# A hybrid decoder step on one core: the prompt's compressed branch beside the compression, in a buffer that later holds half of u

## The chip, the cores and the metric

One core of a Trainium2 chip runs the kernel. The metric is the device time of one execution in microseconds; the kernel before takes 1119.47 us (median of 3 runs, 1118.45 to 1124.41).

## What is computed

The kernel is one inference step of a one-layer hybrid decoder for T = 320 tokens in float32: a prompt of 256 and 8 samples of 8 tokens with caches. Shortened, the reference is:

```python
q, kv, ag, z, xbc, dt, mg = split(rmsnorm(x) @ w_in)         # 1024 -> 6 kinds of columns
A = NSA(q, kv, ag)      # three branches per head, each its own softmax, summed with sigmoid gates
#   o_c: 15 compressed blocks of 32 tokens (a small MLP over the raw keys and values: "compression")
#   o_s: selected 64-token blocks       o_w: a sliding window of 512
M = Mamba2(z, xbc, dt)  # causal conv of width 4, chunked SSD scan, gated norm
h = x + (sigmoid(ga) * (A @ Wa) + sigmoid(gm) * (M @ Wm)) @ w_out
y = h + HierMoE(rmsnorm(h))   # 4 groups of 8 experts: best group, then the best 2 experts in it
```

For the prompt, o_c is softmax(q KC + bias) VC over the compressed keys KC, one softmax row for each token, each of 16 heads; the bias carries ALiBi and the mask.

## The kernel before, in words

Tokens lie on the free axis (320 columns) wherever a projection is computed: a 256-column block of w_in comes in as `w`, ACT and DVE split it into a high and a low part (`whl`, `split`, L342 and L343), and PE multiplies by `xh` and `xl` in three products of 128x128 by 128x320 per 128 rows (`mm`, 24 for a tile of 128 output columns). These projections are the filler of the whole first half: the generator `st_fill` yields 16 conv tiles (`post_xbc`), 8 z tiles (`post_z`), then merge gates and the two output branches. A function `_drive(main, fill, rate)` runs main generators and the filler on a virtual clock (each `yield` is a cost in ns; the filler's are multiplied by a rate), which sets the order in which the program is written; the scheduler of the tile framework then fixes each engine's order. Nothing is reordered at run time: an engine whose next instruction waits holds all that stands behind it.

The stages, with their places in the trace: k, v, q projections (0 to about 92 us); `st_cmp`, the compression of eight samples and the prompt (to about 225); `st_prompt`, the prompt's attention (to about 310); `st_att`, the samples' attention (to about 421); `st_ssd` (to about 562); output projection and router; `ph_moe` from about 645 on, whose weights come over the SP queue through a ring of buffers.

- The head of `st_prompt` is the compressed branch: 16 products of q with `KC` into a PSUM tile (`at`), bias added on DVE (L944), row maximum (L945, L946), subtract (L947), multiply by the slopes (L951), Exp on ACT (L952), sum (L953), reciprocal (L776, L777), gates (L956), scaling (L959), 8 transposes on PE and two copies (L965) into `PcT`. All of it works in `Pc`, one of three buffers of the tag `PP`.
- The main loop of `st_prompt` has 16 turns (head pair r, query tile qt): `probs` multiplies q2 and K2 (`at<-K,q`, in high and low parts), adds the mask with a row maximum on DVE (`ttr`, L782; L994 scales the maxima) and takes four Exps on ACT (L998); `norm` scales (DVE, and POOL at L1008); `out` transposes `PP`, copies, and multiplies by the values (`pv`) together with `PcT`.
- `ph_b_setup` makes K2 (ACT L646, DVE L648) just before; `q2_parts` makes the two parts of q2 (ACT L655, POOL L656).
- `st_ssd` begins by transposing `u`, the conv's x half, which the filler wrote to memory (`ud`) and `ph_c_setup` loads back on ACT's DMA queue (L1153).
- `st_att` begins with DMAs on the SP queue: a constant row `cB` (L790), `P` (L794), then the windows (`wraw`, L799).
- `back` in the MoE transposes the one-hot rows `oh` of an expert and, with three products with N = 3 in float32 each, fetches the expert's coefficients `cr`; six small copies put them in place.

Of the kernel before, what the change touches and what calls it, by code (L numbers as in the profile page):

```python
# [9 lines left out]
F32 = mybir.dt.float32  # L10
# [22 lines left out]
T = 320  # L33
# [132 lines left out]
class _Body:  # L166
# [288 lines left out]
    def ph_a(s):  # L455
# [174 lines left out]
    def ph_b_setup(s):  # L630
# [39 lines left out]
    def st_cmp(s):  # L670
# [14 lines left out]
        for pr in range(4):  # L685
            n = 256 if pr else 292
            for kv in range(2):
# [54 lines left out]
                if pr == 0:  # L742
# [59 lines left out]
    def st_att(s):  # L802
# [4 lines left out]
        def one(b):  # L807
# [65 lines left out]
            def ptb(srcs):  # L873
# [3 lines left out]
                t = s.tl(P_, [128, 4, 128], F32, "PT", bufs=8)  # L877
# [20 lines left out]
            tn = s.tl(P_, [128, 4, 128], F32, "PT", bufs=8)  # L898
# [29 lines left out]
    def st_prompt(s):  # L928
# [3 lines left out]

        Pc = s.Pc
        Pv = Pc.rearrange("p (a n) -> p a n", n=32)
        stt = s.tl(P_, [128, 3, 32], F32, "cst")
        KC = s.KC.rearrange("p g n -> p (g n)")
        for qt in range(2):
            p = s.ps("at", [128, 512])
            if qt == 1:
                s.q2_parts(0, 2)  # L940
            for r in range(8):
                n = 96 if r < 7 else 64
                s.mm(p[:, r * 64:r * 64 + n], s.qT[:, r, qt * 128:(qt + 1) * 128], KC[:, 0:n], True, True)
            nc.vector.tensor_tensor(Pc[:, qt * 512:(qt + 1) * 512], p, Pc[:, qt * 512:(qt + 1) * 512], op=OP.add)  # L944
        nc.vector.tensor_reduce(stt[:, 0], Pv, axis=AX.X, op=OP.max)  # L945
        nc.vector.tensor_scalar(stt[:, 0], stt[:, 0], -1e20, None, op0=OP.max)  # L946
        nc.vector.tensor_tensor(Pv, Pv, stt[:, 0, :, None].to_broadcast([128, 32, 32]), op=OP.subtract)  # L947
        psl = s.ca("psl")
        for qt in range(2):
            v = Pv[:, qt * 16:(qt + 1) * 16]  # L950
            nc.vector.tensor_tensor(v, v, psl[:, :, None].to_broadcast([128, 16, 32]), op=OP.mult)  # L951
        nc.scalar.activation(Pc, Pc, AF.Exp)  # L952
        nc.vector.tensor_reduce(stt[:, 1], Pv, axis=AX.X, op=OP.add)  # L953
        s.recip_gate(None, stt[:, 1], None)
        for qt in range(2):
            nc.vector.tensor_tensor(stt[:, 2, qt * 16:(qt + 1) * 16].rearrange("p (r g) -> p r g", g=2),  # L956
                                    stt[:, 1, qt * 16:(qt + 1) * 16].rearrange("p (r g) -> p r g", g=2),
                                    gp[:, qt, :, :, 0].rearrange("p g r -> p r g"), op=OP.mult)
        nc.vector.tensor_tensor(Pv, Pv, stt[:, 2, :, None].to_broadcast([128, 32, 32]), op=OP.mult)  # L959
        PcT = s.tl(P_, [128, 8, 128], F32, "PcT")  # L960
        for hh in range(2):
            p = s.ps("tp", [128, 4, 128])
            for u in range(4):
                s.tr(p[:, u], Pc[:, (hh * 4 + u) * 128:(hh * 4 + u + 1) * 128])
            nc.scalar.copy(PcT[:, hh * 4:hh * 4 + 4], p)  # L965
        yield 4500
        sl = _slopes()
        nsl = s.ca("nsl")
        def probs(r, qt):
# [89 lines left out]
    def st_fill(s):  # L1059
# [27 lines left out]
        def late():  # L1087

            n = 344
            if pend:  # L1090
# [17 lines left out]
                if f % 4 == 3:  # L1108
                    q = f // 4
                    pt = s.ps("tp", [32, 4, 128])  # L1110
                    for k in range(4):
                        s.tr(pt[:27, k], ctail[:, q * 4 + k])
                    cv = s.tl(P, [27, 512], F32, "cv")
                    nc.scalar.copy(cv, pt[:27].rearrange("p a b -> p (a b)"))
                    nc.sync.dma_start(s.O["conv_prompt"][:, q * 512:(q + 1) * 512], cv[0:3])
                    nc.sync.dma_start(s.O["conv_sample"].rearrange("b w c -> (b w) c")[:, q * 512:(q + 1) * 512], cv[3:27])

        def post_z(m):
            def post(p):
# [5 lines left out]
                nc.sync.dma_start(s.zd[m // 2][m % 2], z)  # L1125
                if m == 7:
# [18 lines left out]

# [951 lines left out]
```

## Time and profile before

| | before |
|---|---|
| time, median of 3 runs | 1119.47 us |
| the profiled execution: its own time, its span | 1119.53 us, 1117.8 us |
| PE busy | 1057.1 us (95%) |
| DVE busy, ACT busy | 618.2 us (55%), 409.6 us (37%) |
| moved by DMA | 298.01 MB, 267 GB/s on average |

Busy time is the time in which an engine has an instruction running; "idle before, releaser" is the time that it stood still ahead of an instruction, with what ended that. PEclk is the granted clock of TensorE as a share of its full 2.4 GHz; a window at 0.50 ran at the lower level, 1.2 GHz, throughout. Outside the span lie 1.7 us of the execution.

### The profile page before, as it was taken

The numbers are of one execution on the slowest core, as the hardware profiler recorded it, in microseconds if no ns is written. First come the engines' busy times: TensorE is split into PE (matmuls) and PEld (weight loads), VectorE is DVE, ScalarE is ACT, GpSimd is POOL, SyncE is SP. The second block draws the span as 40 slices with busy tenths as digits, with TensorE's granted clock in tenths as the row PEclk, the third lists the DMA queues.
The fourth block names the chain that finished last, engine by engine and source line by source line (L and its number), as shares of the span: only waits on it lengthen the run. The fifth ranks groups of instructions, "written<-read, shape, count | busy, mean of one in ns | idle before, by whom it ended". The sixth has DMA issues, their size and how long they took to land.

```text
span 1117.8 us, 18377 instructions
## 1 busy us (share of the span) xinstructions
PE 1057.1 (95%) x6743; PEld 728.9 (65%) x6743; DVE 618.2 (55%) x1686; ACT 409.6 (37%) x959; POOL 85.0 (8%) x115
## 2 busy tenths in 40 slices
PE   6998999969999998999999989999999999999997
PEld 6898899957776787777899944354444444435333
DVE  4467777788867774578876532333434333333324
ACT  4446565677745452545545511110101010101101
POOL 3102000042200001024100000000000000000000
PEclk8999999989999998999999999999999999999999
DMA  7844555511266656584579969999999999999995
GB/s 213 229 139 141 164 153 155 149 56 55 87 181 204 196 153 191 155 229 91 138 267 342 375 211 411 413 414 413 411 412 414 413 414 413 412 412 414 413 413 197
DMA packets 141742, 298.01 MB, mean 267 GB/s; under 512 B 14918, under 2 KB 93222, under 8 KB 133970
## 3 DMA queue, kind: packets, MB, share of 16 engines
q1 hardware_dynamic: 135146, 283.34, 70.7%
q0 software_dynamic: 2688, 7.91, 2.3%
q10 hardware_dynamic: 3816, 5.56, 1.6%
q8 instruction: 55, 0.90, 0.3%
q14 instruction: 37, 0.30, 0.1%
HBM read 279.63 MB, written 15.29 MB: 264 GB/s over the span
## 4 chain that ended last, share of the span: by engine, by line


## 5 line engine op out<-in xcount | busy, mean ns | idle before, releaser
L215 PE MATMUL mm<-xh,whl 128*128 128x320 f32 (+1 forms) x1008 | 248.8, 326 | 7.6 <-ACT whl L342 4.4
L215 PEld LDWEIGHTS mm<-xh,whl 128*128 128x128 f32 (+1 forms) x1008 | 173.5, 191 | 21.1 <-issue 7.9
L215 PE MATMUL mm<-wr,xeT 128*64 128x512 f32 x752 | 171.8, 595 | 4.8 <-DMA wr<-in_w_exp_up 3.0
L215 PE MATMUL mm<-xl,whl 128*128 128x320 f32 (+1 forms) x504 | 162.9, 323 | 0.0
L215 PEld LDWEIGHTS mm<-wr,xeT 128*64 128x64 f32 x752 | 53.5, 137 | 109.8 <-issue 103.6
L215 PE MATMUL po<-wr,ehT 128*64 128x512 f32 (+1 forms) x448 | 118.5, 580 | 4.2 <-DMA wr<-in_w_exp_down 4.2
L343 DVE TENSOR_TENSOR whl<-w,whl 128x1024 fp32r<-128x1024 f32 (+1 forms) x79 | 96.0, 1217 | 23.7 <-ACT whl L342 22.5
L1805 DVE SCALAR_TENSOR_TENSOR eth<-eth,mm 128x256 f32<-128x256 f32 x31 | 13.1, 421 | 170.6 <-ACT eth L1804 170.6
L342 ACT ACTIVATE whl<-w 128x1024 fp32r<-128x1024 f32 (+1 forms) x79 | 83.1, 1055 | 45.8 <-PE mm L215 38.5
L215 PEld LDWEIGHTS mm<-xl,whl 128*128 128x128 f32 (+1 forms) x504 | 96.3, 191 | 3.3 <-issue 1.6
L1804 ACT ACTIVATE eth<-mm,cb 128x256 f32<-128x256 f32 x31 | 14.7, 475 | 201.0 <-PE mm L215 201.0
L215 PEld LDWEIGHTS po<-wr,ehT 128*64 128x64 f32 x448 | 37.3, 137 | 72.3 <-issue 60.3
L1858 DVE TENSOR_TENSOR ht<-sc,ht 128x512 f32<-128x512 f32 (+3 forms) x99 | 61.7, 665 | 38.7 <-PE sc L215 38.2
L215 PE MATMUL mm<-ah,whl 128*128 128x320 f32 x256 | 63.9, 322 | 0.0
L346 DVE SCALAR_TENSOR_TENSOR olo<-po,cb,ohi 128x512 fp32r<-128x512 f32 (+1 forms) x33 | 24.2, 734 | 49.7 <-ACT ohi L345 49.7
L1780 ACT ACTIVATE ohT<-tp 128x320 fp32r<-128x320 f32 x16 | 7.0, 437 | 106.1 <-PE sc L215 98.3
L215 PEld LDWEIGHTS mm<-ah,whl 128*128 128x128 f32 x256 | 43.9, 188 | 2.0 <-issue 0.7
L215 PE MATMUL tp<-oh,hh 128*128 128x256 f32 x192 | 42.2, 292 | 0.0
L215 PE MATMUL sc<-ohi,ohT 128*128 128x512 f32 (+3 forms) x99 | 41.5, 421 | 0.2
L345 ACT ACTIVATE ohi<-po,cb 128x512 fp32r<-128x512 f32 (+1 forms) x33 | 22.2, 674 | 53.1 <-PE po L215 53.1
L215 PE MATMUL mm<-al,whl 128*128 128x320 f32 x128 | 39.6, 309 | 0.0
L215 PEld LDWEIGHTS tp<-oh,hh 128*128 128x128 f32 x192 | 32.9, 188 | 9.0 <-issue 8.1
(491 smaller groups left out, 1895.0 us busy)
## 6 DMA issues: line engine op xcount, KB each, us to landing
wr<-in_w_exp_down SPq DMA_DIRECT2D x50, 1024.0 KB
wr<-in_w_exp_gate SPq DMA_DIRECT2D x98, 512.0 KB
wr<-in_w_exp_up SPq DMA_DIRECT2D x98, 512.0 KB
w<-in_w_in SPq DMA_DIRECT2D x23, 1024.0 KB
raw<-in_cache_kv SPq DMA_DIRECT2D x112, 128.0 KB
w<-in_w_exp_down SPq DMA_DIRECT2D x10, 1024.0 KB
whl<-in_w_exp_gate SPq DMA_DIRECT2D x20, 512.0 KB
whl<-in_w_exp_up SPq DMA_DIRECT2D x20, 512.0 KB
```

The costliest lines, as they stand in the source:

```text
L215: return s.nc.tensor.matmul(out, lhsT, rhs, start=start, stop=stop, skip_group_check=True)
L342: s.last_split = [nc.scalar.activation(hi, src, AF.Copy), nc.vector.tensor_tensor(lo, src, hi.bitcast(F32), op=OP.subtract)]
L343: nc.vector.tensor_tensor(lo, src, hi.bitcast(F32), op=OP.subtract)]
L345: nc.scalar.activation(hi, src, AF.Copy, scale=scale)
L346: nc.vector.scalar_tensor_tensor(lo, src, scale, hi.bitcast(F32), op0=OP.mult, op1=OP.subtract)
L1780: nc.scalar.activation(t, p[:, 0:T], AF.Copy)
L1804: nc.scalar.activation(hv, g, AF.Tanh, scale=hrs)
L1805: nc.vector.scalar_tensor_tensor(hv, hv, 1.0, g, op0=OP.add, op1=OP.mult)
L1858: nc.vector.tensor_tensor(y, ps[:m], y, op=OP.add)
```

## The change

It moves the compressed branch of the prompt out of `st_prompt` into a generator of its own, `st_pc`, which runs beside `st_cmp`; puts `Pc`, `PcT` and the small `cst` into one tile `ux` of pool pU, which is later allocated again for `u`, loaded by `load_x` on the SP queue; makes parts 2 to 7 of q2 later, each pair behind an Exp; saves SBUF at five places to make room; and in `back` takes `cr` in two fp32r parts. Cut to its core ("..." is what is left out; the body of `st_pc` between the products and the transposes is the removed code, word for word but for the tile and a `yield` after each step or two):

```diff
 def post_q(r):
-    t = s.tl(s.pst, [128, T], F32, "qt", bufs=2)
+    t = s.tl(s.pst, [128, T], F32, "kvx", bufs=2)
...
-    si.append(s.tl(s.pst, [24, 1024], F32, "si", bufs=2))
+    si.append(s.tl(s.pst, [128, 1024], F32, "xscr", bufs=3)[:24])
...
+    def ph_pc_setup(s):
+        t = s.tl(s.pU, [128, 8 * T], F32, "ux")
+        s.Pc = t[:, 0:1024]
+        s.PcT = t[:, 1024:2048].rearrange("p (a b) -> p a b", b=128)
+        s.cst = t[:, 2048:2144].rearrange("p (a b) -> p a b", b=32)
...
+        nc.sync.dma_start(s.Pc, s.I["cB"][:, o:o + n])
+    def st_pc(s):
+        yield lambda: "kc" in s.flags
...
+        for qt in range(2):
+            p = s.ps("tp", [128, 512])
+            for r in range(8):
+                n = 96 if r < 7 else 64
+                s.mm(p[:, r * 64:r * 64 + n], s.qT[:, r, qt * 128:(qt + 1) * 128], KC[:, 0:n], True, True)
+            nc.vector.tensor_tensor(Pc[:, qt * 512:(qt + 1) * 512], p, Pc[:, qt * 512:(qt + 1) * 512], op=OP.add)
+            yield 3000
...
+        for hh in range(2):
+            p = s.ps("tp", [128, 4, 128])
+            for u in range(4):
+                s.tr(p[:, u], Pc[:, (hh * 4 + u) * 128:(hh * 4 + u + 1) * 128])
+            nc.scalar.copy(s.PcT[:, hh * 4:hh * 4 + 4], p)
+            yield 3000
-    def q2_parts(s, a, b):
+    def q2_parts(s, a, b, after=None):
...
+            with s.tc.issue_after(after.ins) if after is not None else nullcontext():
+                s.nc.scalar.activation(hi, q, AF.Copy)
...
-        t = s.tl(s.pB, [128, 292], F32, "gt", bufs=2)[:, :n]
+        t = s.tl(s.pB, [128, 292], F32, "gt")[:, :n]
...
-                t = s.tl(P_, [128, 4, 128], F32, "PT", bufs=8)
+                t = s.tl(P_, [128, 4, 128], F32, "PT", bufs=6)
...
     def st_prompt(s):
-        Pc = s.Pc
...
+        PcT = s.PcT
+        s.q2_parts(0, 2)
...
         for r in range(8):
             for qt in range(2):
+                cur = probs(r, qt)
                 if r % 2 == 0 and qt == 1 and r < 6:
-                    s.q2_parts(r + 2, r + 4)
-                cur = probs(r, qt)
+                    s.q2_parts(r + 2, r + 4, s.last_exp)
...
-                if f % 4 == 3:
+                if f % 2:
...
-                    cv = s.tl(P, [27, 512], F32, "cv")
+                    cv = s.tl(P, [27, 256], F32, "cv")
...
         def post_z(m):
...
+                if "prompt" in s.flags:
+                    s.load_x()
...
+    def load_x(s):
+        if not hasattr(s, "u"):
+            s.u = s.tl(s.pU, [128, 8 * T], F32, "ux").rearrange("p (f t) -> p f t", t=T)
+            for k in range(2):
+                s.nc.sync.dma_start(s.u[:, 4 * k:4 * k + 4], s.ud[k].rearrange("f p t -> p f t"))
     def ph_c_setup(s):
+        s.load_x()
...
-        for k in range(2):
-            nc.scalar.dma_start(s.u[:, 4 * k:4 * k + 4], s.ud[k].rearrange("f p t -> p f t"))
...
+        s.crs = s.tl(P, [128, 3, 16, 2, 3], F32R, "crs")
+        s.split(s.crs[:, :, :, 0], s.crs[:, :, :, 1], s.cr)
...
-                mm(p[:, 384:387], o[i], s.cr[:, i, e // 2], i == 0, i == 2)
+                mm(p[:, 384:390], o[i], s.crs[:, i, e // 2].rearrange("p a b -> p (a b)"), i == 0, i == 2)
...
-                nc.vector.tensor_copy(cb[u, 0:1], p[u, 384 + a:385 + a])
+                nc.vector.tensor_reduce(cb[u, 0:1], p[u, 384 + a:390:3], axis=AX.X, op=OP.add)
...
-    _drive([s.st_cmp()], [fill], RATES[0])
+    s.ph_pc_setup()
+    _drive([s.st_cmp(), s.st_pc()], [fill], RATES[0])
...
     _drive([s.st_prompt()], [fill], RATES[3])
+    s.flags.add("prompt")
```

How the orders of the engines change, at three places. The names are those of the tiles; numbers behind them tell copies of a tile apart.

**PE where the prompt's attention begins.** Before, the first transposes of `PP` are those of the compressed branch (two rows of four), behind the products of three turns:

```order
L215 MATMUL at_2527<-K_317_2339,q_316_2338 128x512 x2
L215 MATMUL at_2608<-K_317_2339,q_316_2338 128x256 x4
L215 MATMUL at_2657<-K_317_2339,q_316_2338 128x512 x2
L215 MATMUL mm_4017<-xh_119,whl_3763 128x320 x2
L215 MATMUL mm_4017<-xl_120,whl_3763 128x320
L215 MATMUL mm_4017<-xh_119,whl_3763 128x320
L227 MATMUL tp_2389<-cA_109,PP_2336 128x128 x4
L227 MATMUL tp_2395<-cA_109,PP_2336 128x128 x4
L227 MATMUL tp_2446<-cA_109,ctail_1097 27x128 x4
```

In the change:

```order
L215 MATMUL mm_3741<-xh_119,whl_3621 128x320
L215 MATMUL at_2408<-K_323_2390,q_322_2389 128x256 x2
L215 MATMUL at_2476<-K_323_2390,q_322_2389 128x512 x2
L215 MATMUL at_2408<-K_323_2390,q_322_2389 128x256 x2
L215 MATMUL mm_3987<-xh_119,whl_3738 128x320
L215 MATMUL mm_3987<-xl_120,whl_3738 128x320
L215 MATMUL at_2479<-K_323_2390,q_322_2389 128x512 x2
L215 MATMUL at_2519<-K_323_2390,q_322_2389 128x256 x4
L215 MATMUL at_2615<-K_323_2390,q_322_2389 128x512 x2
L215 MATMUL at_2618<-K_323_2390,q_322_2389 128x512 x2
L215 MATMUL mm_3987<-xh_119,whl_3738 128x320 x2
L227 MATMUL tp_2501<-cA_109,PP_2406 128x128 x4
```

The products with `KC` and the eight transposes of the branch are gone from here (they now stand between the `hh` products of the compression), and the first transposes are those of the main loop's first turn, `PP_2406`. Ahead of the first `at<-K,q` stand 44 products of the filler since the last transposes of the compression.

**DVE in the compression, change.** The operations of the branch (on `ux`) stand between the conv's (`cvt`, `ut`) and the gelu's (`gt`, `gx`) of the compression:

```order
L671 TENSOR_TENSOR ux_984<-tp_1475,ux_984 128x512
L1114 SCALAR_TENSOR_TENSOR ut_2609<-raw_2607,cvt_2451 128x256
L673 TENSOR_REDUCE ux_984<-ux_984 128x32
L1115 SCALAR_TENSOR_TENSOR ut_2609<-raw_2607,cvt_2451 128x64
L674 TENSOR_SCALAR ux_984<-ux_984 128x32
L1090 MEMSET raw_2680 128x3
L676 TENSOR_TENSOR ux_984<-ux_984 128x1024
L714 SCALAR_TENSOR_TENSOR gt_1560<-gt_1560,gx_1558 128x256
L681 TENSOR_TENSOR ux_984<-ux_984,cA_11_110 128x512
L716 SCALAR_TENSOR_TENSOR gx_1558<-gt_1560,gx_1558 128x256
L681 TENSOR_TENSOR ux_984<-ux_984,cA_11_110 128x512
```

What was one block at the head of `st_prompt` is now spread over the second half of the compression, one step ahead of or behind each step of the other streams.

**ACT in the tail of st_ssd.** Before, one Tanh table serves the gates `gm`, and the table for Ln and Exp is loaded once behind them:

```order
L1477 ACTIVATE gm_5306<-mm_6384 128x320
L1350 ACTIVATE k_1002_6416<-at_6410 64x4x64
L1393 ACT_TABLE_LOAD
L1398 ACTIVATE ysq_6280<-ysq_6297 128x320
L1350 ACTIVATE k_1005_6437<-at_6431 128x512
L342 ACTIVATE whl_6457<-w_6299 128x1024
L342 ACTIVATE whl_6521<-w_6378 128x1024
```

In the change a third gate stands behind that load, and the tables are changed again from there on:

```order
L1503 ACTIVATE gm_5298<-mm_6370 128x320
L342 ACTIVATE whl_6399<-w_6335 128x1024
L1376 ACTIVATE k_1008_6434<-at_6428 64x4x64
L1419 ACT_TABLE_LOAD
L1376 ACTIVATE k_1011_6455<-at_6449 128x512
L1503 ACT_TABLE_LOAD
L1503 ACTIVATE gm_5298<-mm_6402 128x320
```

In the whole program the change has 18 rows of ACT_TABLE_LOAD where there were 11; the 7 new ones all stand from this place to the end of `st_ssd`. On the SP queue the first half of `u` now stands directly ahead of `cB`, `P` and the windows, and it writes the tile that the last `pv` of `st_prompt` reads.

## Rows read from the trace of the kernel before

**Rows 1.** Windows, head of st_prompt: length, busy PE PEld DVE ACT POOL, PEclk, DMA.
```profile
230.00:255.00 25.00, 13.67 (x70) 11.15 (x70) 23.14 (x53) 16.31 (x39) 14.48 (x10) 0.73 0.15 48
245.00:250.00 5.00, 2.05 (x6) 1.35 (x6) 5.00 (x21) 3.59 (x17) 0.41 (x1) 0.50 0.00 0
250.00:255.00 5.00, 4.18 (x19) 3.64 (x20) 5.00 (x13) 1.44 (x4) 2.17 (x2) 0.53 0.67 207
```
**Rows 2.** Waits of PE, 200 to 260 us: total, times, longest.
```profile
PE at L215 <- DVE pmx L782: 5.9, 2, 4.2
```
**Rows 3.** Timeline of PE there: start, us, instruction, [idle before].
```profile
225.29 0.46 PE L215 MATMUL mm<-xh,whl 128*128 128x320 f32 x2
226.61 0.46 PE L215 MATMUL mm<-xh,whl 128*128 128x320 f32 x2
227.05 3.68 PE L215 MATMUL at<-KC,qT 128*128 128x96 f32 x32
252.25 1.94 PE L227 MATMUL tp<-cA,PP 128*128 128x128 f32 x8 [0.21 <-DVE PP L959]
```
**Rows 4.** Timeline of ACT there.
```profile
224.68 1.28 ACT L440 ACT_TABLE_LOAD   x1
225.97 0.69 ACT L440 ACTIVATE cr<-tp,small 128x512 f32<-128x512 f32 x1
228.89 2.56 ACT L646 ACTIVATE K<-kvT 64x512 fp32r<-64x512 f32 x4
231.48 5.22 ACT L655 ACTIVATE q<-qT 64x512 fp32r<-64x512 f32 x8
244.72 0.40 ACT L998 ACTIVATE PP<-PP,pmx 128x128 f32<-128x128 f32 x1
```
**Rows 5.** Timeline of POOL there.
```profile
232.25 12.42 POOL L656 TENSOR_TENSOR q<-qT,q 64x512 fp32r<-64x512 f32 x8 [28.90 <-ACT q L655]
```
**Rows 6.** Timeline of DVE there.
```profile
229.78 2.78 DVE L648 TENSOR_TENSOR K<-kvT,K 64x512 fp32r<-64x512 f32 x4
232.59 1.29 DVE L944 TENSOR_TENSOR PP<-at,PP 128x512 f32<-128x512 f32 x2
237.94 2.26 DVE L947 TENSOR_TENSOR PP<-PP,cst 128x1024 f32<-128x1024 f32 x1
243.47 1.22 DVE L994 TENSOR_TENSOR pmx<-pmx,cA 128x4 f32<-128x4 f32 x1
247.61 0.14 DVE L994 TENSOR_TENSOR pmx<-pmx,cA 128x4 f32<-128x4 f32 x1
250.47 1.63 DVE L959 TENSOR_TENSOR PP<-PP,cst 128x1024 f32<-128x1024 f32 x1
254.80 1.21 DVE L343 TENSOR_TENSOR whl<-w,whl 128x1024 fp32r<-128x1024 f32 x1
```
**Rows 7.** Windows, the compression from 160 us on.
```profile
160.00:225.00 65.00, 64.80 (x507) 61.73 (x506) 47.12 (x117) 38.84 (x105) 0.78 (x7) 1.00 0.51 150
```
**Rows 8.** Windows, the start of st_ssd.
```profile
430.00:445.00 15.00, 10.49 (x65) 9.54 (x63) 5.68 (x10) 1.79 (x4) 0.00 (x0) 0.77 0.57 168
```
**Rows 9.** Timeline of PE there.
```profile
437.07 1.08 PE L227 MATMUL tp<-cA,u 128*128 128x128 f32 x4 [4.51 <-DMA u<-ud]
```
**Rows 10.** Timeline of the SP queue, end of st_prompt.
```profile
310.40 0.33 SPq L794 DMA_DIRECT2D P<-in_cB  x1
```
**Rows 11.** Timeline of DVE: first reader of cB's row.
```profile
314.03 0.22 DVE L782 CUSTOM_DVE_ANT_0 pn<-at,cB 128x64 f32<-128x64 f32 x1
```
**Rows 12.** Windows: tail of st_ssd, and the MoE.
```profile
551.00:570.00 19.00, 19.00 (x138) 17.49 (x138) 14.49 (x27) 8.94 (x15) 1.25 (x2) 1.00 0.47 150
667.00:1050.00 383.00, 379.25 (x1924) 172.15 (x1922) 134.83 (x307) 50.56 (x96) 0.00 (x0) 1.00 1.02 412
```
**Rows 13.** Waits of the SP queue, 600 to 720 us.
```profile
SPq L1434 <- PE mm L215: 36.6, 15, 11.8
```
**Rows 14.** Instructions on tile cr, by line and form: min/median/max ns.
```profile
L215 PE MATMUL tp<-cr,oh x96: 170/252/253, 659.5 to 1071.0; 128*128 128x3 f32 x96
```

More of the change, by code (lines that the diff above doesn't have):

```diff
@@ L648, in ph_b_setup @@
                 nc.vector.tensor_tensor(s.K2[R[h], 1, g], k, s.K2[R[g], 0, g].bitcast(F32), op=OP.subtract)
-    def q2_parts(s, a, b):
+    def ph_pc_setup(s):
+        nc = s.nc
+        t = s.tl(s.pU, [128, 8 * T], F32, "ux")
+        s.Pc = t[:, 0:1024]
+        s.PcT = t[:, 1024:2048].rearrange("p (a b) -> p a b", b=128)
+        s.cst = t[:, 2048:2144].rearrange("p (a b) -> p a b", b=32)
+        o, n = s.bo["pC"]
+        nc.sync.dma_start(s.Pc, s.I["cB"][:, o:o + n])
+    def st_pc(s):
+        nc = s.nc
+        yield lambda: "kc" in s.flags
+        Pc, stt = s.Pc, s.cst
+        Pv = Pc.rearrange("p (a n) -> p a n", n=32)
+        gp = s.gtok.rearrange("p i (g r c) -> p i g r c", g=2, c=3)
+        KC = s.KC.rearrange("p g n -> p (g n)")
+        b3 = [128, 32, 32]
+        for qt in range(2):
[5 more added lines that the diff above has]
+            yield 3000
+        nc.vector.tensor_reduce(stt[:, 0], Pv, axis=AX.X, op=OP.max)
+        nc.vector.tensor_scalar(stt[:, 0], stt[:, 0], -1e20, None, op0=OP.max)
+        yield 4000
+        nc.vector.tensor_tensor(Pv, Pv, stt[:, 0, :, None].to_broadcast(b3), op=OP.subtract)
+        yield 4000
+        psl = s.ca("psl")
+        for qt in range(2):
+            v = Pv[:, qt * 16:(qt + 1) * 16]
+            nc.vector.tensor_tensor(v, v, psl[:, :, None].to_broadcast([128, 16, 32]), op=OP.mult)
+            yield 3000
+        nc.scalar.activation(Pc, Pc, AF.Exp)
+        yield 4000
+        nc.vector.tensor_reduce(stt[:, 1], Pv, axis=AX.X, op=OP.add)
+        s.recip_gate(None, stt[:, 1], None)
+        for qt in range(2):
+            nc.vector.tensor_tensor(stt[:, 2, qt * 16:(qt + 1) * 16].rearrange("p (r g) -> p r g", g=2),
+                                    stt[:, 1, qt * 16:(qt + 1) * 16].rearrange("p (r g) -> p r g", g=2),
+                                    gp[:, qt, :, :, 0].rearrange("p g r -> p r g"), op=OP.mult)
+        yield 4000
+        nc.vector.tensor_tensor(Pv, Pv, stt[:, 2, :, None].to_broadcast(b3), op=OP.mult)
+        yield 6000
+        for hh in range(2):
[3 more added lines that the diff above has]
+            nc.scalar.copy(s.PcT[:, hh * 4:hh * 4 + 4], p)
+            yield 3000
@@ L750, in st_cmp @@
                     if kv:
+                        s.flags.add("kc")
                         for i in range(4):
@@ L931, in st_prompt @@
         gp = s.gtok.rearrange("p i (g r c) -> p i g r c", g=2, c=3)
-        Pc = s.Pc
[L934 to L966, printed above, removed]
+        PcT = s.PcT
+        s.q2_parts(0, 2)
         sl = _slopes()
@@ L997, in probs @@
                     k = g * 2 + br
-                    nc.scalar.activation(blk(br, g), blk(br, g), AF.Exp, bias=mx[:, 1, k:k + 1], scale=float(sl[g * 8 + r]),
-                                         accum_out=mx[:, 2, k:k + 1])
+                    s.last_exp = nc.scalar.activation(blk(br, g), blk(br, g), AF.Exp, bias=mx[:, 1, k:k + 1],
+                                                      scale=float(sl[g * 8 + r]), accum_out=mx[:, 2, k:k + 1])
             return r, qt, P, mx, blk
@@ L1107, in late @@
                         nc.scalar.dma_start(s.ubc[:, 4 * k:4 * k + 4], s.ud[2 + k].rearrange("f p t -> p f t"))
-                if f % 4 == 3:
[L1109 to L1112, printed above, removed]
-                    cv = s.tl(P, [27, 512], F32, "cv")
+                if f % 2:
+                    q = f // 2
+                    pt = s.ps("tp", [32, 2, 128])
+                    for k in range(2):
+                        s.tr(pt[:27, k], ctail[:, q * 2 + k])
+                    cv = s.tl(P, [27, 256], F32, "cv")
                     nc.scalar.copy(cv, pt[:27].rearrange("p a b -> p (a b)"))
-                    nc.sync.dma_start(s.O["conv_prompt"][:, q * 512:(q + 1) * 512], cv[0:3])
-                    nc.sync.dma_start(s.O["conv_sample"].rearrange("b w c -> (b w) c")[:, q * 512:(q + 1) * 512], cv[3:27])
+                    nc.sync.dma_start(s.O["conv_prompt"][:, q * 256:(q + 1) * 256], cv[0:3])
+                    nc.sync.dma_start(s.O["conv_sample"].rearrange("b w c -> (b w) c")[:, q * 256:(q + 1) * 256], cv[3:27])
         def post_z(m):
@@ L1144, in st_fill @@
         yield from s.proj(groups, then)
+    def load_x(s):
+        if not hasattr(s, "u"):
+            s.u = s.tl(s.pU, [128, 8 * T], F32, "ux").rearrange("p (f t) -> p f t", t=T)
+            for k in range(2):
+                s.nc.sync.dma_start(s.u[:, 4 * k:4 * k + 4], s.ud[k].rearrange("f p t -> p f t"))
     def ph_c_setup(s):
         nc = s.nc
+        s.load_x()
         s.pG = s.pool("pG")
@@ L1772, in back @@
             p = s.ps("tp", [128, 392])
-            o = [oh[:, i].bitcast(F32).rearrange("p a b -> p (a b)") for i in range(3)]
+            o = [oh[:, i].rearrange("p a b -> p (a b)") for i in range(3)]
             for i in range(3):
-                tr(p[:, i * 128:(i + 1) * 128], o[i])
+                tr(p[:, i * 128:(i + 1) * 128], o[i].bitcast(F32))
             for i in range(3):
-                mm(p[:, 384:387], o[i], s.cr[:, i, e // 2], i == 0, i == 2)
+                mm(p[:, 384:390], o[i], s.crs[:, i, e // 2].rearrange("p a b -> p (a b)"), i == 0, i == 2)
             t = s.tl(P, [128, T], F32R, "ohT", bufs=2)
```

9 lines of the change are left out of this document (2 added, 7 removed).

## The prediction, on record before the change was run

> **What bounds the kernel now.** I read the windows first, to find where PE, 95% busy, stands still; then what it waited for there; then the timelines of the engines in those places; last what bounds the MoE. Two holes stand out ahead of the MoE.
>
> The first lies at the head of `st_prompt`: in 25 us PE is busy for 13.67, so it is idle for 11.3, and the granted clock falls to 0.50 and 0.53 [rows 1], its lower level. Work done there took longer than at the full clock: 2.05 x 0.50 + 4.18 x 0.47 = 3.0 us. The hole costs 14.3 us. Most of its idle time is 5.9 us for a row maximum on DVE [rows 2]; DVE is 23.14 of 25 us busy [rows 1]. What it does is the compressed branch: thirteen operations, of which the first two, one in the middle and the last stand in [rows 6]; by line, from L944 to L959, they take 12.2 us (1.29 + 1.22 + 0.59 + 2.26 + 3.21 + 1.21 + 0.17 + 0.34 + 0.26 + 1.63). PE gets no further than two turns of the main loop, and its first transposes, at 252.25, are released by the last of them [rows 3].
>
> The second lies at the start of `st_ssd`: PE waits 4.51 us for `u` from memory [rows 9], and the window around it has 10.49 us of work at a mean clock of 0.77, a loss of 10.49 x 0.23 = 2.4 us [rows 8]. It costs 6.9 us.
>
> From 667 us on the MoE is bound by its loads: DMA share 1.02 for 383 us [rows 12]. Time won earlier counts only if the loads start earlier too. They do: in 600 to 720 us the SP queue waits 36.6 us for PE to give buffers free [rows 13], so a PE that comes earlier moves the loads with it, one for one. I pass every shift on in full.
>
> **The change, part by part.** The sum stands against the profiled execution, 1119.53 us (span 1117.8, 1.7 around it), which is 0.06 over the median of 1119.47.
>
> *Head of the prompt's attention: -5 us (0 to -14.3).* The branch's DVE work goes, so the hole could lose all of its 14.3 us. But the next thing is late at once: K2 and q2. The chain starts with the compression's last transposes at about 224: table load 224.68, K2 on ACT from 228.89 for 2.56 us [rows 4], its low parts on DVE until 232.6 [rows 6]. q2 needs two of the eight ACT copies (5.22 / 8 = 0.65 each) [rows 4], to 232.8, and two of eight subtractions on POOL (12.42 / 8 = 1.55 each) [rows 5], to about 235.7. PE has 44 products ahead of its first `at<-K,q` in the change's order; nine of them take 226.61 - 225.29 = 1.32 us, 0.147 each [rows 3], so they cover 6.5 us, to about 231. PE then idles some 1.6 us for K2's low part, runs 0.8 us, and some 2.3 us for q2's. After that come the maxima, four Exps of about 0.3 us each in a row (0.40 for one with its start-up [rows 4]), sums and scaling, some 5 us to the first transposes, against about 4 us of products for the turns ahead: 1 us idle, as much again for the second turn, and 1 for conv work that stands on ACT between q2 and the Exps. That is 7; as the hole is shorter I take 2 for the clock, less than the 3.0 above. 9.3 of 14.3 stay. The ends are the hole gone and the hole as long as before.
>
> *`KC` products and transposes: 0.* The products take 3.68 us [rows 3] in either place; the eight transposes took 1.94 at half the clock [rows 3], and the 1 us to be had from that is in the hole's clock loss already.
>
> *The branch on DVE in the compression: +1 us (0 to +15).* DVE is busy for 47.12 of the 65 us there and PE for 64.80 [rows 7], so there is no slack on PE and 18 us on DVE. Beside POOL the operations were slow: the same L994 took 1.22 us at 243.47, within POOL's eight subtractions [rows 5], and 0.14 at 247.61, after them [rows 6]; a subtract of 128x1024 took 2.26 within them and a split of the same shape 1.21 at 254.80, with POOL done [rows 6]. POOL is busy for 0.78 us in the compression [rows 7], so I price L947, L951 and L959 at 1.2 instead of 2.26, 3.21 and 1.63, and the branch at 8.7. DVE comes to 55.8 of 65 us (86%); with 12.2 us it would be 59.3 (91%). The gelu (`gt`, `gx`) and the filler's splits stand in order behind steps of 1.2 us, and PE waits for both; the transposes of the compression wait for the gelu. I take one such delay; the upper end is the whole 12.2 us on PE and a clock loss like the 3.0 above. The Trainium skill, "SBUF — State Buffer", section "SBUF: two separate sides", says that a VectorE operation with two SBUF inputs and a GpSimd operation that reads SBUF exclude each other for the whole instruction; the pairs of rows agree. By it the branch costs the 8.7, without it 12.2 and the term would be some 0.5 more.
>
> *q2's other six subtractions beside the main loop: +0.5 us (0 to +6.5).* Each may hold up a short DVE operation by 1.22 - 0.14 = 1.08 us [rows 6], in the loop's chain from maximum to Exp. Six would be 6.5. Most will fall beside other work. It is the same rule as above, and here it speaks against the change.
>
> *`u`: -5.5 us (-3.5 to -6.9).* It is issued behind the last `pv` with `ux`, at about 309, and read 120 us later. The hole of 6.9 us goes but for what is late next there, the other loads and transposes of the same stage; 1.4 for that.
>
> *Start of the samples' attention: +1 us (0 to +3).* SP's order now has half of `u`, which waits for that `pv`, ahead of `cB`. `P`, which also waited for the prompt's end, went out at 310.40 [rows 10]; `cB` will go out at about 309.5 behind 0.65 MB. Its first reader runs at 314.03 [rows 11]. Both together are 128 x (1280 + 1864) x 4 bytes, 1.6 MB, 6 us at the run's average of 267 GB/s, so `cB` lands at about 315.5 and DVE starts 1.5 us late; the windows behind it are late by as much. Products of the filler cover a part; twice the delay is the upper end.
>
> *Tail of `st_ssd`: +1.5 us (0 to +2.5).* Seven more table loads are 7 x 1.28 = 9.0 us of ACT [rows 4], of which the last ones stand in the chain of the norm that the last branch waits for; PE was full there, 19.00 of 19 us [rows 12], with 46 products behind the last transposes, and has 28 now: 18 x 0.147 = 2.6 us less cover. What follows a load starts at once: 224.68 + 1.28 = 225.96, and the next instruction starts at 225.97 [rows 4]. The Trainium skill, "ScalarE: Activation LUTs", section "What ACT_TABLE_LOAD costs", adds a drain of about 1.38 us to each switch; by that it would be 18.6 us of ACT instead of 9.0 and this term about 1 us more. The row shows none.
>
> *The start: +0.3 us (0 to +1.2).* The loads of `state_conv` now wait on ACT's queue until PE has transposed the x tiles whose buffers they take, and ACT's next work behind them; no row shows it, and I bound it by one step such as DVE's split of 1.21 us [rows 6]. *`back`: -0.3 us (-1.4 to 0).* 96 products of 128x3 took up to 0.25 us each [rows 14], six columns in fp32r are fewer passes; but beside loads at 1.02 [rows 12] only the first few experts count.
>
> Sum: -5 + 1 + 0.5 - 5.5 + 1 + 1.5 + 0.3 - 0.3 = -6.5, so 1119.53 - 6.5 = **1113.0 us**.
>
> **The rivals.** *The whole first hole goes* (chance 0.20). For it: 5.9 us of its waits are for DVE [rows 2], and 44 products stand ahead. Against it: K2 and q2 end after those. Then 9.3 us less: about 1104.
>
> *The hole only changes its cause* (0.20). PE waits for q2's low parts on POOL and then for Exps that stand behind conv work on ACT as long as it waited for DVE; or the six late subtractions hold the loop by their 6.5 us. For it: ACT was busy 16.31 of 25 us [rows 1]. Then about 5 us less is won: 1118. The page on SBUF named above would have it so if each of the six met such an operation.
>
> *The branch holds up the compression* (0.11), the slower end: on DVE, between 160 and 225 us, each of its steps puts off a gelu or a split for which PE waits, and PE's clock falls. 12.2 + 3.0 us instead of 1: 1113 + 14 = 1127. It decides from some 12 us of new waits on. Against it: the 18 us that DVE has free there [rows 7].
>
> *The MoE takes nothing over* (0.04): if its loads were not tied to PE, the time would stay at 1119.5. The 36.6 us [rows 13] speak against it. That the change would not do what it says can be left out: the order shows the branch moved and `u` early.
>
> **How the numbers follow.** My forecast has 0.45, with a range of its own of 1109.5 to 1116.5. A difference of 0.5%, 5.6 us, is about what a measurement can tell from none, so faster means under 1113.9 and slower over 1125.1. Of the forecast's 0.45, 0.28 lie under 1113.9; with the 0.20 of the first rival faster has 0.48. The rest of it, 0.17, and the second and last rivals, 0.24, make no change 0.41; slower is 0.11. The range of 1104 to 1120 leaves out the slower rival and the lower part of the first.
>
> **What would show it.** Right: no DVE lines of the branch after 225 us; PE idle some 6 to 7 us between 225 and 250, for K2, q2 and Exps; no wait for `u`; small waits for gelu or splits between 160 and 225; up to 2 us for `cB` or windows at 310 to 320; the weights' loads some 6 us earlier. Wrong: a wait over 5 us at a new place, a low clock in the compression, or PE idle in the tail of `st_ssd` for over 3 us.

## The result

The change takes 1114.57 us (median of 11 runs) against 1120.48 us of the kernel before beside it (11 runs). One run of the change took 3548.31 us and is left out of the ratio. The ratio is 0.9938, 95% interval 0.9919 to 0.9957: 6.9 us faster by the ratio, 5.9 by the medians, where 6.5 were forecast. Run once more with the later experiments it had 0.9942 (0.9927 to 0.9958). The sum was right, its parts were not. By the profiles the head of the prompt's attention gave 4.8 us less than forecast and the tail of `st_ssd` cost 6.7 us more, and a gain of 5.7 us that stood in no term made up for half of that. So the number is in good part luck.

The profiled execution took 1116.08 us, span 1114.3. Four stages of the trace, first of the kernel before, then of the change (columns as in [rows 1]):

```profile
95.00:130.00 35.00, 30.10 (x193) 27.79 (x193) 30.05 (x66) 23.94 (x58) 6.78 (x15) 0.90 0.44 134
225.00:300.00 75.00, 63.66 (x489) 49.18 (x487) 65.80 (x260) 57.00 (x178) 24.73 (x22) 0.91 0.16 51
425.00:450.00 25.00, 20.49 (x137) 19.21 (x137) 13.01 (x23) 7.27 (x16) 1.97 (x3) 0.86 0.59 174
550.00:600.00 50.00, 50.00 (x348) 47.88 (x348) 37.03 (x61) 21.95 (x34) 1.25 (x2) 1.00 0.78 261
```

```profile
95.00:130.00 35.00, 32.48 (x234) 30.53 (x233) 29.89 (x73) 25.74 (x63) 0.34 (x3) 1.00 0.53 154
225.00:300.00 75.00, 66.40 (x484) 48.84 (x482) 63.62 (x265) 57.81 (x193) 23.70 (x23) 0.91 0.14 44
425.00:450.00 25.00, 25.00 (x176) 21.72 (x175) 16.19 (x44) 12.66 (x26) 0.00 (x0) 1.00 0.56 144
550.00:600.00 50.00, 43.76 (x276) 41.84 (x276) 28.75 (x45) 20.56 (x31) 2.99 (x3) 0.93 0.75 259
```

In the first row PE's idle time falls from 4.9 to 2.5 us and the clock from 0.90 goes to 1.00; in the third both losses vanish; in the last the change loses 6.2 us and clock where the kernel before lost nothing; and the second, the hole that the branch was moved for, has 2.7 us less idle time and no better clock. To add idle time and clock, I take each 5 us window's idle time plus busy time x (1 - PEclk), and sum by stage, up to 700 us:

| stage, us | before: idle + clock | change: idle + clock | difference |
|---|---|---|---|
| 0 to 95 | 11.9 + 4.9 | 11.9 + 4.6 | -0.3 |
| 95 to 130 | 4.9 + 3.3 | 2.5 + 0.0 | -5.7 |
| 130 to 225 | 0.4 + 0.0 | 0.6 + 0.0 | +0.2 |
| 225 to 300 | 11.3 + 3.3 | 8.6 + 5.8 | -0.2 |
| 300 to 425 | 2.1 + 0.0 | 1.1 + 0.0 | -1.0 |
| 425 to 450 | 4.5 + 2.5 | 0.0 + 0.0 | -7.0 |
| 450 to 550 | 4.5 + 0.0 | 3.4 + 1.2 | +0.1 |
| 550 to 600 | 0.0 + 0.0 | 6.2 + 2.0 | +8.2 |
| 600 to 700 | 5.2 + 0.0 | 5.0 + 0.0 | -0.2 |

Together -5.9 us. Two of the three large terms are not where I put them: a gain between 95 and 130 us that no step foresaw, and a loss at 550 to 600 us several times the one that I priced.

**The head of the prompt's attention.** What PE waits for there now, between 225 and 310 us (total, times, longest):

```profile
PE tp L227 <- DVE PP L1029: 3.8, 4, 2.0
PE at L215 <- POOL q L707: 2.5, 3, 1.7
PE mm L215 <- DVE whl L343: 1.1, 1, 1.1
PE at L215 <- DVE pmx L834: 0.8, 1, 0.8
```

The branch is gone from the list, and what was said to be late next is there: q2 from POOL, maxima, the scaled `PP`. A wait for K2, forecast at 1.6 us, is not. The clock, after that:

```profile
240.00:245.00 5.00, 3.02 (x24) 2.35 (x24) 5.00 (x15) 2.70 (x11) 3.93 (x3) 1.00 0.00 0
245.00:250.00 5.00, 5.00 (x32) 3.70 (x31) 3.31 (x16) 3.29 (x9) 0.66 (x1) 0.53 0.00 0
250.00:255.00 5.00, 5.00 (x33) 3.31 (x31) 3.10 (x19) 2.76 (x13) 0.49 (x1) 0.79 0.02 6
```

PE is idle for 2.0 of the 5 us to 245, and then runs almost at the lower level for 5 us and partly for 5 more, though it is never idle in them.

**The end of st_ssd.** Here stands the new hole, with two waits in a row on PE, and just before it ACT's last norm:

```profile
565.63 0.41 PE L215 MATMUL mm<-xh,whl 128*128 128x320 f32 x1 [2.56 <-ACT whl L342]
569.32 1.09 PE L227 MATMUL tp<-cA,ht 128*128 128x128 f32 x4 [3.13 <-DMA ht<-in_x_prompt]
```

```profile
548.82 1.28 ACT L1420 ACT_TABLE_LOAD   x1
550.64 0.53 ACT L1420 ACTIVATE ysq<-tp,small 128x320 f32<-128x320 f32 x1 [0.54 <-PE tp L215]
551.18 1.28 ACT L1421 ACT_TABLE_LOAD   x1
552.48 0.47 ACT L1421 ACTIVATE ysq<-ysq 128x320 f32<-128x320 f32 x1
```

The Ln and the Exp of one row of norms, 0.53 and 0.47 us, now have a table load of 1.28 us each ahead of them. The first of the two waits on PE ends with a split of weights on ACT. That split stands in order behind two copies of `gm`, which waited 3.16 and 2.61 us for DVE; the second of them, and the split:

```profile
564.16 0.47 ACT L345 ACTIVATE ah<-gm 128x320 fp32r<-128x320 f32 x1 [2.61 <-DVE gm L1550]
564.54 1.99 ACT L342 ACTIVATE whl<-w 128x1024 fp32r<-128x1024 f32 x2
```

### The profile page after: what moved, and what is told of

The parts are those of the page before. It is cut to its first block, busy times and chain, and to the rows that moved or that the text cites. A ratio compares the mean times of both kernels' runs of the same rounds, so it can differ in the third digit from the quotient of the medians.

```text
span 1114.3 us, 18300 instructions
## 1 busy us (share of the span) xinstructions
PE 1057.2 (95%) x6695; PEld 725.0 (65%) x6695; DVE 616.2 (55%) x1687; ACT 419.6 (38%) x971; POOL 76.8 (7%) x115
## 4 chain that ended last, share of the span: by engine, by line
## 5 line engine op out<-in xcount | busy, mean ns | idle before, releaser
L215 PE MATMUL mm<-wr,xeT 128*64 128x512 f32 x752 | 174.1, 595 | 5.1 <-DMA wr<-in_w_exp_up 3.2
L215 PE MATMUL po<-wr,ehT 128*64 128x512 f32 (+1 forms) x448 | 122.2, 588 | 6.2 <-DMA wr<-in_w_exp_down 6.2
L215 PE MATMUL sc<-ohi,ohT 128*128 128x512 f32 (+3 forms) x99 | 41.5, 421 | 0.2
```

Of the source, the lines that this page charges most:

```text
L215: return s.nc.tensor.matmul(out, lhsT, rhs, start=start, stop=stop, skip_group_check=True)
```

## The experiments

Every ratio is to the kernel before, run beside it, with its 95% interval.

**The scratch tags alone.** In the kernel before:

```diff
-                t = s.tl(s.pst, [128, T], F32, "qt", bufs=2)
+                t = s.tl(s.pst, [128, T], F32, "kvx", bufs=2)
...
-                        si.append(s.tl(s.pst, [24, 1024], F32, "si", bufs=2))
+                        si.append(s.tl(s.pst, [128, 1024], F32, "xscr", bufs=3)[:24])
```

> The kernel before with two lines of the change alone: the q tiles take the tag kvx, and the two loads of state_conv take buffers of xscr; nothing of the branch, of u, of q2 or of the MoE. Theory (space): in the kernel before, POOL's memset of pc waits 41.5 us, to 94.65, for an address that a scratch tile holds; two tags fewer put pc where the memory is free earlier. So the memset starts near 58 us, the 2.40 us wait of PE at 103 us and the low clock behind it go, and the time is 4 to 6 us under the kernel before. Rival (order): the wait went because the filler was emitted in another order; then this kernel keeps the memset at 94 us and is within 1 us of before.

Measured 0.9971 (0.9957 to 0.9985), 3.2 us faster. POOL's memset of `pc`, in the kernel before, in the change, and here:

```profile
94.65 0.93 POOL L677 MEMSET pc<- 128x704 f32 x1 [41.52 <-ACT w1h L342]
```

```profile
58.18 0.68 POOL L728 MEMSET pc<- 128x704 f32 x1 [4.25 <-DMA out_win_sample<-kvtok]
```

```profile
59.21 0.69 POOL L677 MEMSET pc<- 128x704 f32 x1 [4.41 <-DMA out_win_sample<-kvtok]
```

And the stage here:

```profile
95.00:130.00 35.00, 32.46 (x234) 30.50 (x233) 30.32 (x74) 26.25 (x63) 0.34 (x3) 1.00 0.48 148
```

PE's wait in this stage for what ACT makes of `pc`, in the kernel before and here:

```profile
PE hh L215 <- ACT ch L342: 2.4, 1, 2.4
```

```profile
PE hh L215 <- ACT ch L342: 0.6, 1, 0.6
```

The stage is that of the change: the theory of space holds for the place and the cause. Its size came out smaller than expected: the stage gives 5.7 us in the profiles, the runs 3.2 (1.7 to 4.8).

**u loaded late.**

```diff
-                if "prompt" in s.flags:
-                    s.load_x()
```

> The change without its early load of u: load_x is called in ph_c_setup only, still on the SP queue. Theory (u exposed): PE waits 4 to 6 us for u again at the start of st_ssd with a low clock behind it, and the time is 5 to 8 us over the change. Rival (hidden anyway): the stage has other late loads, so less than 2 us over the change.

Measured 0.9994 (0.9978 to 1.0011), some 6 us over the change, but the experiment missed what it was for. The loads, by the view of the tile `ux`:

```profile
L1170 SPq DMA_DIRECT2D ux<-ud x2: 803/940/1076, 302.5 to 384.8; - x2
```

The first still goes out at 302.5 us: with the tile free, the scheduler puts it ahead by itself. PE never waits for u, so the time says nothing about it. Its trace loses 2.5 us more than the change between 300 and 425 us, all of it clock, and 3.4 us more between 450 and 550 us, where PE now waits 1.8 us for a load of `h` and 2.0 us for a split. Why this order has them is open.

**The branch back at the head.**

```diff
-    _drive([s.st_cmp(), s.st_pc()], [fill], RATES[0])
+    _drive([s.st_cmp()], [fill], RATES[0])
...
+        for _ in s.st_pc():
+            pass
         PcT = s.PcT
```

> The change with the compressed branch back at the head of st_prompt (the same generator, run there without yields; its tile, its early load and everything else stay). Theory (a new wait took the place): in the change the first turns wait for q2, K2, maxima and Exps and the clock falls as long as before, so the move itself is worth little: within 2 us of the change. Rival (the recorded forecast's reading): the branch's 12.2 us of DVE come back into the hole: 4 to 6 us over the change.

Measured 1.0021 (1.0004 to 1.0038): 9 us over the change, more than either theory. Its profiled execution, 1118.2 us, was the fastest of its 12 and shows a loss of 14.4 us at the head, like the change; the mean granted clock of its runs was 0.978, against 0.982. This order also has the 18 table loads. By the 0.9 us for each 0.001 of clock that is found below, the lower clock is some 3 us (an estimate); where the rest lies the one trace can't tell. A second try stands below.

**The filler held back.**

```diff
-RATES = (6, 3, 1.1, 1)
+RATES = (6, 3, 2.0, 1)
```

> The change with one number: in st_ssd the filler's cost is taken 2.0 times instead of 1.1, so that fewer of its products go into st_ssd: 1445 of 2416 stand ahead of the last norm's transposes instead of 1484, and the first transposes of ht stand behind 1704 instead of 1562. Theory (no filler left): the hole of the change at 560 to 575 us (5.7 us idle, 2 to 3 us of low clock) closes, and the time is 5 to 8 us under the change. Rival (moved): PE idles inside st_ssd instead, between 450 and 550 us, by as much; within 2 us of the change.

Measured 0.9966 (0.9950 to 0.9981): 3 us over the change, with overlapping intervals. The windows:

```profile
450.00:550.00 100.00, 92.79 (x619) 77.22 (x617) 69.77 (x134) 53.55 (x86) 20.63 (x23) 0.97 0.53 139
550.00:600.00 50.00, 48.75 (x328) 47.43 (x327) 34.25 (x54) 25.36 (x38) 2.57 (x3) 1.00 0.87 286
```

The hole at 550 to 600 us closes nearly, and PE is idle for 7.2 us ahead of it instead, where the change has 3.4. The rival holds in kind, the idle time was mostly moved; by the time the run lies somewhat above its 2 us.

**The change again.**

> The change itself once more, for a comparison on the same chip as the runs beside it: ratio 0.992 to 0.996 to the kernel before.

Measured 0.9942 (0.9927 to 0.9958), as expected; the next three were run beside it.

**q2 without POOL.**

```diff
-            s.nc.gpsimd.tensor_tensor(s.q2[R[1 - g], g, a:b], q, hi.bitcast(F32), op=OP.subtract)
+            s.nc.vector.tensor_tensor(s.q2[R[1 - g], g, a:b], q, hi.bitcast(F32), op=OP.subtract)
```

> The change with the low parts of q2 subtracted on DVE instead of POOL (all eight). Theory (POOL's q2 is the new wait at the head): PE waits 2.5 us for q2 from POOL there, and short DVE operations take 0.8 to 1.24 us beside POOL's second pair (0.13 to 0.17 without), which makes the 1.99 us wait for the scaled PP. Without POOL those waits fall to under 1 us each and part of the 5.8 us of low clock with them: 2 to 5 us under the change. Rival (DVE is the bound of the main loop, 90% busy there): the six later subtractions, 0.7 us each, delay its chain: within 1 us of the change, or slower.

Measured 0.9958 (0.9940 to 0.9976): not faster than the change. What the theory says of POOL is there in the change's trace. DVE, then POOL:

```profile
238.22 0.16 DVE L1023 TENSOR_TENSOR pmx<-pmx,gtok 128x4 f32<-128x4 f32 x1
242.23 0.82 DVE L1023 TENSOR_TENSOR pmx<-pmx,gtok 128x4 f32<-128x4 f32 x1
243.32 1.35 DVE L1029 TENSOR_SCALAR PP<-PP,pmx 128x256 f32<-128x256 f32 x2
```

```profile
240.06 2.97 POOL L707 TENSOR_TENSOR q<-qT,q 64x512 fp32r<-64x512 f32 x2
```

The same operation on 128x4 takes 0.16 us at 238 and 0.82 us at 242, where it ends with POOL's subtractions for q2's second pair (242.23 + 0.82 and 240.06 + 2.97 us). The Trainium skill, "SBUF — State Buffer", section "SBUF: two separate sides", would have it so, as the operation has two SBUF inputs. Another operation on the same tile, L828, takes 0.17 us at 237.03 and 1.24 us at 240.18. But without POOL PE waits for other things:

```profile
PE tp L227 <- DVE PP L1029: 2.2, 6, 0.7
PE pv L215 <- ACT PPT L1039: 1.8, 2, 1.1
PE at L215 <- DVE q L707: 1.3, 1, 1.3
```

The rival holds as to the time. In the one trace the head loses 8.1 us idle and 3.0 us of clock instead of 8.6 and 5.8, as the theory would have it; the 12 runs don't show that gain.

**The transposes of ht held back**, behind the sixth tile of the last branch (`fm5` is its last product):

```diff
...
+            with s.tc.issue_after(s.fm5.ins) if f < 2 else nullcontext():
                 for i, m in enumerate(NT):
                     s.tr(xT[:, i * 128:i * 128 + m], ht[:m, i, f * 128:(f + 1) * 128], m)
```

> The change with the first transposes of ht held back on PE behind the sixth tile of the last branch (they stand behind 1704 products again, as before the change, instead of 1562). Theory: the 3.1 us wait for the load of ht goes and with it the low clock after it, while the 2.6 us wait for the split of the last branch's weights stays: 2 to 5 us under the change. Rival (the weights are just as late): PE waits for the weights instead, within 1 us of the change.

Measured 0.9908 (0.9891 to 0.9925): 3.8 us under the change. PE's two longest waits between 540 and 600 us in the change are the 3.13 us for `ht` and the 2.56 us for the split that are shown above; the longest here:

```profile
PE mm L215 <- ACT whl L343: 2.9, 2, 2.6
```

The wait for `ht` is gone, that for the weights' split stays. As the theory has it.

**Products that nobody reads, in the 2.0 us gap.**

```diff
...
                     out(*last)
+                    if last[:2] == (0, 0):
+                        s.warm(8, s.last_mm)
```

> The change with eight products of the identity with itself (about 0.23 us each at the full clock; their result is read by nothing) put into PE's 2.0 us wait for the second turn's scaled PP. They take no time from anything if they fit. Theory (the low clock at 245 to 255 us follows from PE standing still before it): the granted clock stays at or near 1.00 there and 2 to 3.4 us are won. Rival (the clock fell for the earlier waits, at 229 to 240): the clock is as low as before and the time within 1 us, or up to 1 us longer.

Measured 0.9980 (0.9967 to 0.9993), 4 us over the change, which neither side expected. The windows of the same place:

```profile
235.00:240.00 5.00, 3.79 (x11) 2.18 (x9) 4.35 (x21) 4.50 (x18) 1.14 (x1) 0.50 0.00 0
240.00:245.00 5.00, 5.00 (x23) 4.27 (x24) 5.00 (x13) 2.73 (x12) 4.22 (x4) 0.50 0.00 0
245.00:250.00 5.00, 5.00 (x49) 4.32 (x48) 4.96 (x17) 4.35 (x13) 0.66 (x1) 0.92 0.05 20
```

The gap is filled, but the clock is 0.50 already from 235 us on, so the eight products ran at the lower level and took longer than the gap; from 245 on the clock is 0.92 where the change had 0.53. So the products came too late to test the theory. The rival isn't shown either: the waits ahead of 240 us are the same in both traces (1.73, 0.4, 0.79 and 1.1 us), but from 235 to 245 us the change has 0.65 and 1.00 where this run has 0.50 twice. Over the whole head the clock costs the same, 5.7 and 5.8 us; when it falls is not explained by these waits alone. The profiled spans differ by 1.3 us only (1115.8, and 1114.5 of the change run beside it).

**One edge on ACT: the table behind the last gate** (`gate7` is the last Tanh).

```diff
             if g == 0:
-                s.tc.keep_in_program_order(nc.scalar.preload_act_table_set("natural_log_exp_and_others"))
+                with s.tc.issue_after(s.gate7.ins):
+                    s.tc.keep_in_program_order(nc.scalar.preload_act_table_set("natural_log_exp_and_others"))
...
```

> The change with one edge on ACT: the early load of the table for Ln and Exp stands behind the last Tanh of the merge gates. ACT then has 11 table loads again instead of 18, and on PE 1464 products stand ahead of the last norm's transposes and 1704 ahead of the first of ht (change: 1484 and 1562). Theory (one gate out of place made the hole at 560 to 575 us): the hole of about 8 us closes, and the time is 4 to 8 us under the change. Rival (the hole is from the weights and the filler, not from ACT's tables): within 2 us of the change.

Measured 0.9876 (0.9854 to 0.9898): 1107.16 us, by the ratios some 7 us under the change and 13.9 under the kernel before, the fastest of all but for one that is equal to it. The table loads of ACT between 421 and 575 us, in the change, then here:

```profile
L1420 ACT ACT_TABLE_LOAD x4 | 5.1, 1283 | 0.1
L1503 ACT ACT_TABLE_LOAD x2 | 2.6, 1283 | 0.0
L1421 ACT ACT_TABLE_LOAD x2 | 2.6, 1283 | 0.0
L1419 ACT ACT_TABLE_LOAD x1 | 1.3, 1283 | 0.0
L1376 ACT ACT_TABLE_LOAD x1 | 1.3, 1283 | 0.0
```

```profile
L1421 ACT ACT_TABLE_LOAD x1 | 1.3, 1283 | 0.0
L1504 ACT ACT_TABLE_LOAD x1 | 1.3, 1283 | 0.0
L1420 ACT ACT_TABLE_LOAD x1 | 1.3, 1283 | 0.0
```

And the windows here, at the head of the prompt and at the end of `st_ssd`:

```profile
225.00:300.00 75.00, 66.36 (x474) 49.10 (x473) 63.15 (x264) 58.61 (x190) 23.20 (x22) 0.91 0.13 44
550.00:600.00 50.00, 50.00 (x342) 49.10 (x341) 34.67 (x57) 24.70 (x46) 2.38 (x3) 1.00 0.89 307
```

The hole is gone in full, 50.00 of 50 us busy at 1.00. The edge does two things, it saves seven loads and lets the scheduler find an order with more products behind the last norm; which of them counts for how much was not tried apart. That holding back `ht` alone gave 3.8 us shows that the order has a part.

**The branch back at the head, in the old code and buffers.** The edit is that of the first try, with the block of the kernel before in place of the generator, `Pc` a `PP` tile again, and `ux` only for u.

> The change with the compressed branch back at the head of st_prompt in the code of the kernel before, word for word, and in its buffers (Pc one of the PP tiles); u's early load, the tags, q2's later pairs and the MoE stay as in the change. This order has 11 table loads and 1704 products ahead of ht, so it is to be held against the run with the table's edge. Theory A (the move is worth something, 4 to 10 us as the first run without it said): 4 to 10 us over that run. Theory B (a new wait took the whole place of the old one, as the two profiles' losses of 14.6 and 14.4 us at the head say): within 2 us of it.

Measured 0.9902 (0.9871 to 0.9934). Its order has no misplaced gate, so it stands against 0.9876: the move is worth 0.0026, 2.9 us, and the intervals overlap. The head here:

```profile
225.00:300.00 75.00, 65.87 (x489) 50.01 (x487) 68.55 (x271) 56.16 (x187) 24.38 (x23) 0.91 0.16 52
```

Its loss by 5 us windows is 9.1 + 5.7 us, against 8.7 + 5.7 in the run with the edge. Theory B fits the trace and the runs allow it; 5 us for the move are not excluded.

**back as before.** The five lines of `back` and the split of `cr` undone.

> The change with back as before: three columns of cr in float32, copies instead of sums. Theory (hidden beside the loads): within 1.4 us of the change. Rival (PE is the bound of the MoE in places): 3 to 8 us over the change.

Measured 0.9953 (0.9934 to 0.9972), 1.2 us over the change run later (0.9942), inside its interval. Hidden, as expected; 3 us, the rival's lower end, are not excluded.

**The edge, and q2's first pair on DVE.** Beside the edge shown above:

```diff
...
-            s.nc.gpsimd.tensor_tensor(s.q2[R[1 - g], g, a:b], q, hi.bitcast(F32), op=OP.subtract)
+            (s.nc.gpsimd if a else s.nc.vector).tensor_tensor(s.q2[R[1 - g], g, a:b], q, hi.bitcast(F32), op=OP.subtract)
```

> The run with the table's edge, and the low parts of q2's first pair subtracted on DVE, which waits there for POOL; the three later pairs stay on POOL. Theory: the first 1.7 us wait for q2 shrinks to under 0.8 and some low clock goes: 1 to 3 us under the run with the edge alone. Rival: the next wait (maxima, Exps) takes it: within 1 us.

Measured 0.9886 (0.9859 to 0.9914), equal to the edge alone. Idle time at the head falls from 8.7 to 7.3 us, the clock's part goes from 5.7 to 6.0: the rival.

## Why the prediction came out right, and where its steps did not

The runs give a ledger, in shares of the time before. Scratch tags: -0.0029. u early, with q2's later pairs, `back` and the smaller savings (the second try with the old head, 0.9902, less the tags): -0.0069. The move of the branch (0.9876 less 0.9902): -0.0026, not separated from zero. The gate out of place (0.9938 or 0.9942 less 0.9876): +0.0062 to +0.0066. They add up to what was measured because each is the difference of two neighbours in one chain of runs from the kernel before to the change; the sum proves nothing. What the ledger shows is the parts, each to within some 0.001 to 0.004, and they are not all my terms: the move that I priced at 5 us is the least certain of them, and the tail took back nearly as much as u and the small parts gave. Of the signs that I named for a wrong forecast one came: PE idle in the tail of `st_ssd` for 6.2 us, over twice the 3 that I allowed.

*Head of the prompt's attention, -5: wrong in size.* The chain that I named is the one that is late next. Idle time stayed near my 7 us: 6.1 between 225 and 250 and 2.5 more in the loop behind it. The mis-sized term is the clock, 5.8 us where I took 2: behind several short waits it was low for longer than behind the one long wait of before, 3.0 [rows 1]. The change's second trace has 5.6, the orders made from it 3.0 to 6.0; why they differ is open. (My parts, 7 and 2, make 9, not the 9.3 that I wrote; the term would have been -5.3.) So 14.4 of 14.6 us stayed, the rival "the hole only changes its cause", for this term.

*The branch on DVE, +1: right, and cheaper.* 0.2 us more loss from 130 to 225. Its operations beside no POOL, by the view of the tile:

```profile
L676 DVE TENSOR_TENSOR ux<-ux x1: 1226/1226/1226, 144.8 to 144.8; 128x1024 f32<-128x1024 f32 x1
L692 DVE TENSOR_TENSOR ux<-ux x1: 1210/1210/1210, 157.3 to 157.3; 128x1024 f32<-128x1024 f32 x1
```

1.23 and 1.21 us where 2.26 and 1.63 had been [rows 6]; 1.2 was taken for each.

*q2's later pairs, +0.5: seen, up to 2 us.* DVE operations were held as the page of the Trainium skill named above has it. Two of them, 1.1 and 0.7 us longer, stand ahead of the 2.0 us wait at 244; taking POOL out gained no time, though.

*u, -5.5: right by the traces.* The stage loses nothing where it lost 7.0. The run with the tags alone keeps the old load, and its PE still waits 3.6 us for `u`, at a loss of 4.9 us in the stage; in none of the traces with the early load does PE wait for it. The experiment meant for its price missed. The ledger's 0.0069, 7.7 us for it with the small parts, is a remainder and fits.

*Start of the samples' attention, +1: nothing came of it.* DVE waits for `cB` as said, half as long as the 1.5 us that I took, and PE has cover: it waits for nothing between 300 and 330 us. The stage's gain of 1.0 us has another place: before 425 us PE waited 1.9 us for DVE (`P`, L893), and waits 0.6 and 0.2 us for others in the change; why is open.

```profile
DVE pn L834 <- DMA cB<-in_cB: 0.7, 1, 0.7
```

*Tail of st_ssd, +1.5 (0 to +2.5): wrong, it cost 8.2 us in the profiles and 7 in the runs.* I saw the seven loads and the 18 products less of cover, and priced each by itself. I left out what stands behind: the splits of the last branch's weights, in ACT's order behind `gm`, and `ht`, whose load begins only when `st_ssd` ends. In the change it is issued at 559.64 us and takes 9.5 us; before, it went out at 566.01 us, but PE had no use for it until 596. I had not seen that the order puts `ht`'s transposes behind 1562 products instead of 1704. As on the row [rows 4], the Exp starts 0.02 us after its load ends (551.18 + 1.28, next at 552.48): no drain is seen here either.

*Not on the list: 5.7 us (3.2 in the runs) between 95 and 130 us.* I read the SBUF savings as room for the new tile. They also moved `pc` to memory that is free 36 us earlier, and ended a wait of POOL, then of ACT, then of PE. It stood in the trace of before as an idle POOL of 41.5 us.

*The start, +0.3, and `back`, -0.3: nothing to be seen.* Up to 95 us PE is idle for 11.9 us in both traces, and `back` as before is 1.2 us slower, inside the interval.

*The MoE takes a shift over: right for its loads.* The last experts' weights are asked for 5.5 us earlier (1072.63 against 1078.13 us), of 5.9 us won up to 700 us. Behind them some 2 us are lost again, where PE waits for the last loads (longest 2.7 us against 1.4), so that the span is 3.5 shorter. With the edge 10.2 us less loss gave a span 10.0 shorter; over all profiles the two differ by up to 3.7 us.

## What to carry to other kernels

When a change frees or moves buffers, look in the trace for engines that wait to write a fresh tile: here such a wait was for the memory's last user, and two tags fewer ended it. Where a program order is found by a scheduler, count the table loads in it: one function out of place made 10 of 3 in 150 us, and a single edge gave back as much as the whole change. A hole of many short waits can cost more clock than one long wait (5.8 against 3.3 us here), so price the clock by the waits that are left, not by the hole's length.

## What the runs showed that I had not expected

The granted clock differs between executions of one program by several microseconds' worth. The change's two profiled executions have the same idle time up to 95 us, 11.9 us, but lose 4.6 and 8.2 us to the clock there. Over the ten runs of its ratio the mean clock lies between 0.978 and 0.986 and the time between 1119.72 and 1108.57 us; a straight line through them has 0.9 us for each 0.001. Differences of 2 or 3 us between single traces can be of that kind.

The clock can fall while PE is never idle. At the start of `st_ssd`, in the run with `ht` held back and in the change:

```profile
415.00:420.00 5.00, 5.00 (x25) 4.98 (x25) 0.28 (x1) 0.81 (x2) 2.85 (x4) 0.50 0.94 266
```

```profile
415.00:420.00 5.00, 5.00 (x44) 4.83 (x44) 0.69 (x1) 1.59 (x4) 2.57 (x4) 1.00 1.00 283
```

Both are busy for 5.00 of 5 us; one is at 0.50, the other at 1.00. In both PE comes there to sixteen products with 8 columns, which take 3.28 us from 414.51 in the first and 1.95 us from 415.73 in the second, and then to some with 128. What decides is open.
